# A fourth buffer of split weights, two small copies on another engine, and a mean one step later, in a two-layer hybrid encoder

## The chip, the core and the metric

The kernel runs on one core of a Trainium2 chip. Its engines work side by side, each through a queue of its own: TensorE (matrix products into the accumulation memory PSUM; in the profile PE, its weight loads PEld), VectorE (DVE), ScalarE (ACT), GpSimd (POOL) and SyncE (SP, which here issues most of the loads). The metric is the device time of one execution in microseconds (us); less is better.

## What is computed

Two layers of an encoder over 272 rows (256 tokens and 16 learned meta rows) of width 2048, all in float32. In each layer, shortened from the reference:

```python
proj = h @ w_in                       # gq gk gv gr glr | nq nk nv
y_gla = _gla_mixer(gq, gk, gv, gr, glr, ...)   # 4 heads, both directions, gated by silu(gr)
y_na  = _na_mixer(nq, nk, nv, rel_bias)        # 16 heads, window 4 x 16 of the token grid + 16 meta keys
h = layer_norm(ALPHA * h + concat(y_gla, y_na) @ w_out)
h = layer_norm(ALPHA * h + square(relu(h @ w_ff1)) @ w_ff2)
```

A GLA head's output is divided by the root of its mean square over 256 columns; that mean is the "head's mean" of the title. The keys and values of the neighbourhood attention have 16 columns for the meta rows; these are the "meta columns".

## The kernel before

**Products.** Every product with a weight is made of float32r parts. A weight tile of 128 x 1024 (`raw`, 512 KB from memory) is split by `halves` into a high part (`wh`, a cast on ScalarE, L218) and a low part (`wl`, a subtraction on VectorE, L219). TensorE multiplies high by high, high by the low part of the activations, and low by high. So each of the 768 tiles costs a load, a cast, a subtraction and, in layer 0, 24 matmuls of 272 columns (`eight`, L253). `raw`, `wh` and `wl` are each a ring of three buffers (the pool `wst`, L71). `weights` (L181) hands out the next tile and first sees to it that two tiles are prepared, the one handed out among them.

**Order of the work.** `by_m` (L317) runs one block of 128 output columns after another: for each it takes two or more weight tiles, and after each tile it calls `pump`, after the last one also an eviction of the sum out of PSUM. `by_k` (L279) runs four blocks at once over the pairs of input blocks; it stands at the start of each layer, at the output projection (from `y`, with `mixed` ahead of each pair) and in the first MLP half. The rest of the layer is written as Python generators, which `pump` (L127) steps on between the weight tiles: a foreground queue `fg` (attention pairs, gates) by one step per call, and a background queue `bg` (the four GLA heads, one after another) by a credit per call, 1.3 while the output gates are made (16 calls), 1.4 during the neighbourhood attention. A step that yields True marks the next one as starting with matmuls; such a step is never the second background step of a call, and during the attention it waits up to twice for a marked foreground step (`meet`). Ahead of group 5, the last four blocks of the attention's projection, the background queue is emptied in one go (L405).

The order on each engine's queue is made by the framework's scheduler from this program: earlier instructions first, but one that is ready sooner may be issued ahead. `issue_after(self.wl)` in `step` holds the VectorE instructions of a step behind the newest subtraction L219.

**A GLA head** (`gla_head`, L580) merges keys, queries and decays over levels (L606 on ScalarE, L615 on VectorE, L617 on GpSimd), makes its scores in two groups of small matmuls (L629 to L690), puts them into `A` and `am`, splits these (L339, L340, L345, L346), and multiplies them by the values (L716 to L720: the head's outputs). Squares (L721), their sum (L725) and its split (`mean`, L976) follow; then two matmuls with a constant matrix make the mean (L983), and `newton` the inverse root.

**A pair of attention heads** takes three blocks: query, key, value. `ev_na` (L524) evicts them: a copy of the token columns on ScalarE (L540), one of the meta columns to both halves on VectorE (L541), two small copies on GpSimd (L544). `na_pair` (L762) makes the scores (L778, L782), adds bias and mask (L787, L789, which empty two PSUM banks), takes the softmax (L754 to L760, into `s`, `pr` and, for the meta queries, `sm`), transposes it (L799, L800), turns values (L805 to L808) and sends the probabilities through memory; `na_out` multiplies them (L851) two pairs later. The banks of the scores and of the products come from one ring of four (`pm`).

Of the kernel before, what the change touches and what calls it, by code (L numbers as in the profile page):

```python
# [7 lines left out]
F32 = mybir.dt.float32  # L8
F32R = mybir.dt.float32r
# [5 lines left out]
P = 128  # L15
D = 2048
DC = D // P
T = 256
NM = 16
L = T + NM  # L20
# [8 lines left out]
NK2 = 48  # L29
NKEY = P + NK2  # L30
# [10 lines left out]
WIDE = 1280  # L41
# [17 lines left out]
class Trunk:  # L59
# [24 lines left out]
    def consts(self):  # L84
        nc, c = self.nc, self.cp
        t = lambda n, s, d=F32: c.tile(s, d, name=n, tag=n)
        t("pad", [P, PAD])
        self.vec = t("vec", [P, DEPTH, 66])
        nc.sync.dma_start(self.vec, self.i["vec"].rearrange("l p v -> p l v"))
        self.ident = t("ident", [P, P])  # L90
        nc.sync.dma_start(self.ident, self.i["ident"])
        self.sel = t("sel", [LRK, 2])
        nc.sync.dma_start(self.sel, self.i["sel"])
        self.qmask = t("qmask", [NM, NK2])
        nc.sync.dma_start(self.qmask, self.i["qmask"])
        self.mask = t("mask", [P, 5, 32], U8)
        raw = self.xr.tile([P, 2, L], F32, name="xraw", tag="xraw", bufs=3)[:, 0, :5 * 32].rearrange("p (l c) -> p l c", l=5)
        nc.sync.dma_start(raw, self.i["mask"])
        nc.gpsimd.tensor_copy(self.mask, raw)
        self.ones = {}  # L100
        for n in (GDV, 4 * P, D):
            self.ones[n] = t(f"ones{n}", [P, P])
            nc.gpsimd.memset(self.ones[n], 1.0 / n)
        self.ones_r = {}
        for n in self.ones:
            self.ones_r[n] = t(f"onesr{n}", [P, P], F32R)
            nc.scalar.copy(self.ones_r[n], self.ones[n])
        self.eps = t("eps", [P, 1])
        nc.gpsimd.memset(self.eps, EPS)
        self.one = t("one", [P, 1])  # L110
        nc.gpsimd.memset(self.one, 1.0)
# [68 lines left out]

    def weights(self):  # L181

        while len(self.ready) < 2:
            self.ready.append(self.made(*next(self.stream, (None, (), None))))
        return self.ready.popleft()

    def made(self, ap, ends, kind):
        if ap is None:
            return None
        nc = self.nc  # L190
        raw = self.wp.tile([P, WB], F32, name="raw", tag="raw")
        wh, wl = (self.wp.tile([P, WIDE], F32R, name=nm, tag=nm) for nm in ("wh", "wl"))
        wh, wl = self.blocks(wh, *HIGHS[kind]), self.blocks(wl, *LOWS[kind])
        for c in map(slice, (0,) + ends, ends):
            self.asked = nc.sync.dma_start(raw[:, c], ap[:, c]).ins
            self.halves(raw[:, c], wh, wl, slice(c.start // P, c.stop // P))
        if not ends:
            self.head(ap, raw, wh, wl)
        return wh, wl
# [324 lines left out]
    def ev_na(self, j, ps):  # L524

        nc, m = self.nc, j % 3
        src = ps[:, :T].rearrange("p (r t w) -> p t r w", t=2, r=ROWS)
        if m == 0:
            t = self.a2.tile([P, L], F32, name="nq", tag="nq")
            nc.scalar.mul(t[:, NM:].rearrange("p (t r w) -> p t r w", t=2, r=ROWS), src, NAD ** -0.5)  # L530
            if self.full:
                nc.vector.tensor_scalar(t[:, :NM], ps[:, T:], NAD ** -0.5, None, ALU.mult)
            self.nqkv = [t]
            return
        if m == 1:
            t = self.a2.tile([P, 2, NKEY], F32, name="nk", tag="nk")
            own, rest = t[:, :, :P], t[:, :, P:]
        else:
            t = own, rest = self.nv[j // 3 % 2]
        nc.scalar.copy(own.rearrange("p t (r w) -> p t r w", r=ROWS), src)  # L540
        nc.vector.tensor_copy(rest[:, :, 32:NK2], ps[:, None, T:L].to_broadcast([P, 2, NM]))  # L541
        grid = lambda a: a.rearrange("p (r w) -> p r w", r=ROWS)
        for h, lo in ((0, 0), (1, 24)):
            nc.gpsimd.tensor_copy(grid(rest[:, h, :32]), grid(own[:, 1 - h, :])[:, :, lo:lo + 8])  # L544
        self.nqkv.append(t)
        if m == 2:
            self.y[8 + j // 3] = self.pair(self.yp, "y", 8 + j // 3)
            self.fg.append(self.na_pair(j // 3, *self.nqkv))
            self.wants[self.fg[-1]] = True
# [187 lines left out]
    def na_tiles(self):  # L737

        def t(name, *shape):
            a = self.a2.tile(list(shape), F32, name=name, tag=name, bufs=1)  # L740
            self.nc.gpsimd.memset(a, 0.0)
            return a

        self.fetch = lambda: None
        self.nv = [(self.a2.tile([P, 2, P], F32, name=f"nv{i}", tag=f"nv{i}", bufs=1), t(f"nr{i}", P, 2, 64))
                   for i in range(2)]
        self.npr = [t(f"npr{i}", P, 4, 64) for i in range(2)]
        if self.full:
            self.npm = [t(f"npm{i}", P, 2, NM) for i in range(2)]
            self.nms = [t(f"nms{i}", P, 2, 64) for i in range(2)]  # L750

    def softmax(self, s, st, u, outs, by):
        nc = self.nc
# [8 lines left out]
    def na_pair(self, c, q, k, v):  # L762
        nc, b = self.nc, self.a2
# [2 lines left out]
        bias = b.tile([P, 4, 192], F32, name="nb", tag="nb").rearrange("p u c -> p (u c)")[:, :4 * NKEY]  # L766
        bias = bias.rearrange("p (u c) -> p u c", u=4)
        nc.sync.dma_start(bias, self.i["nab"][self.l, c])
        s = b.tile([P, 4, NKEY], F32, name="ns", tag="ns")
        st = b.tile([P, 12], F32, name="nst", tag="nst")  # L770
        if len(self.due) > 1:
            self.due.popleft()()
        ps = self.spare(2)
        for t in range(2):
            for hh, hs in enumerate(heads):
                for part in heads:
                    at = NM + t * P + part.start
                    nc.tensor.matmul(ps[hh][part, t * NKEY:t * NKEY + NKEY], lhsT=q[hs, at:at + NAD], rhs=k[hs, t, :],  # L778
                                     start=True, stop=True)
        if self.full:  # L780
            for hh, hs in enumerate(heads):
                nc.tensor.matmul(ps[hh][:NAD, 2 * NKEY:2 * NKEY + NK2], lhsT=q[hs, :NAD], rhs=k[hs, 0, P:],  # L782
                                 start=True, stop=True)
            meta = self.nms[c % 2]
            sm = meta[:NM, :, :NK2]
        for hh in range(2):
            nc.vector.tensor_tensor(s[:, 2 * hh:2 * hh + 2, :], two(ps[hh][:, :2 * NKEY]), bias[:, 2 * hh:2 * hh + 2, :], ALU.add)  # L787
            if self.full:
                nc.vector.tensor_tensor(sm[:, hh, :], ps[hh][:NM, 2 * NKEY:2 * NKEY + NK2], self.qmask, ALU.add)  # L789
        pr = self.npr[c % 2]  # L790
        self.softmax(s, st, 4, ((s[:, :, :P], s[:, :, :P]), (pr[:, :, :NK2], s[:, :, P:])), nc.gpsimd)
        yield
        if self.full:
# [26 lines left out]
        p = []  # L820
# [155 lines left out]
    def mean(self, src, n, i=0, pool=None):  # L976

        parts = [t[:, :src.shape[-1]] for t in self.pair(pool or self.lp, "sp", i)]
        self.split(src, *parts)
        yield True  # L980
        p = self.bank()[:, :src.shape[-1]]
        for i, v in enumerate(parts):
            self.nc.tensor.matmul(p, lhsT=self.ones_r[n], rhs=v, start=i == 0, stop=i == 1)  # L983
        return p

    def means(self):
# [140 lines left out]
    def ln_out(self):  # L1127
# [2 lines left out]


        nc, lp, acc = self.nc, self.lp, self.acc
        ident, one = self.ident, self.ones[D]
        t = lambda nm, s, d=F32: lp.tile(s, d, name=nm, tag=nm)
        blocks = [(g, h) for g in range(4) for h in range(2)]
        bank = [self.pm.tile([P, 512], F32, name="mm", tag="mm") for _ in range(4)]
# [145 lines left out]
```

## Time and profile before

| what | us |
|---|---|
| median of 3 runs | 2323.82 (2321.75 to 2325.22) |
| the profiled execution | 2323.91 |
| its span, first to last instruction | 2322.1 |
| TensorE busy | 2304.2 (99%) |
| VectorE busy | 1526.4 (66%) |
| ScalarE busy | 1223.0 (53%) |
| GpSimd busy | 155.4 (7%) |

The profiled execution is 1.8 us longer than its span, and within 0.1 us of the median. A busy TensorE need not be at its peak: a matmul's row in the trace is longer than the distance between the starts of two matmuls, so they overlap. In rows of the timeline stand the start, the length, the engine with its line, what is written from what, its size, and in brackets the idle time before it with what ended it. A line with "q" (SPq, ACTq) is of a queue that issues, not of an engine at work. The granted clock (PEclk) is TensorE's, as a share of its full one.

### The profile page before, as it was taken

The page shows a single profiled execution, that of the slowest core. Times are in us where ns is not written, and L with a number is a line of the kernel's source. Part 1 is how long each engine was busy: PE and PEld are TensorE (multiplying, and loading weights), DVE is VectorE, ACT ScalarE, POOL GpSimd, SP SyncE. Part 2 cuts the span into 40 slices and gives each one's busy share as a digit, 9 for nine tenths or more (in the row PEclk, how much of TensorE's full clock was granted, in tenths as well). Part 3 has the DMA queues.
Part 4 walks back from the last instruction along what each step waited for, and adds up shares of the span by engine and source line. Part 5 has one row for each costly group of instructions (what it writes and reads, how often), then busy time and mean ns, then how long its engine had stood idle before and what let it go on. Part 6 is the DMA issues. An engine that isn't in the chain of part 4 may idle for free.

```text
span 2322.1 us, 45272 instructions
## 1 busy us (share of the span) xinstructions
PE 2304.2 (99%) x18420; PEld 2188.9 (94%) x18420; DVE 1526.4 (66%) x2408; ACT 1223.0 (53%) x2096; POOL 155.4 (7%) x232
## 2 busy tenths in 40 slices
PE   9999999999999999999999999999999999999998
PEld 9999999999999999999999899889988888888888
DVE  5588878875544455547576788688866555666655
ACT  5666655564433344444456766655654334555443
POOL 0023210100000000000020122200100000000000
PEclk9999999999999999999999999999999999999999
DMA  8556666565555556665655556665666666667664
GB/s 259 155 164 184 199 189 177 173 181 181 182 181 178 179 181 182 180 179 178 182 173 173 173 175 209 195 187 181 198 191 196 194 191 193 192 196 218 195 195 150
DMA packets 129824, 431.65 MB, mean 186 GB/s; under 512 B 14792, under 2 KB 23496, under 8 KB 129616
## 3 DMA queue, kind: packets, MB, share of 16 engines
q1 hardware_dynamic: 127024, 421.95, 59.9%
q10 hardware_dynamic: 2592, 6.82, 0.8%
q8 instruction: 144, 2.36, 0.4%
q14 instruction: 64, 0.52, 0.1%
HBM read 420.32 MB, written 8.39 MB: 185 GB/s over the span
## 4 chain that ended last, share of the span: by engine, by line
PE 91%; DVE 5%; ACT 2%; issue 1%; DMA 1%; POOL 0%; DVEq 0%; ACTq 0%; SPq 0%
PE mm L253 53%; PE mm L265 29%; PE mm L304 4%; PE mm L314 2%; DVE wl L219 1%; PE bg L304 1%; ACT wh L218 1%; ACT ns L756 0%; DVE S L615 0%; PE bg L851 0%; PE bg L470 0%; PE bg L629 0%; DVE acc L1085 0%; POOL dec L617 0%; DMA raw<-in_wff 0%
## 5 line engine op out<-in xcount | busy, mean ns | idle before, releaser
L219 DVE TENSOR_TENSOR wl<-raw,wh 128x1024 fp32r<-128x1024 f32 (+1 forms) x770 | 935.9, 1223 | 621.8 <-ACT wh L218 518.5
L218 ACT CAST wh<-raw 128x1024 fp32r<-128x1024 f32 (+1 forms) x770 | 804.7, 1047 | 755.8 <-PE mm L253 352.6
L253 PE MATMUL mm<-x,wh 128*128 128x272 f32 (+3 forms) x4544 | 806.8, 294 | 0.0
L253 PEld LDWEIGHTS mm<-x,wh 128*128 128x128 f32 x4544 | 648.0, 188 | 15.5 <-issue 0.8
L253 PE MATMUL mm<-x,wl 128*128 128x272 f32 (+3 forms) x2432 | 520.6, 285 | 2.9 <-DVE wl L219 2.9
L253 PEld LDWEIGHTS mm<-x,wl 128*128 128x128 f32 x2432 | 391.4, 188 | 3.4 <-DVE wl L219 3.4
L253 PE MATMUL mm<-y,wh 128*128 128x272 f32 (+1 forms) x1440 | 235.0, 285 | 0.0
L253 PEld LDWEIGHTS mm<-y,wh 128*128 128x128 f32 x1440 | 199.7, 188 | 0.1
L265 PE MATMUL mm<-x,wh 128*128 128x512 f32 x832 | 193.8, 390 | 0.0
L265 PEld LDWEIGHTS mm<-x,wh 128*128 128x128 f32 x832 | 154.3, 188 | 31.0
L253 PE MATMUL mm<-u,wh 128*128 128x272 f32 (+1 forms) x1056 | 172.1, 285 | 0.0
L265 PE MATMUL mm<-y,wh 128*128 128x512 f32 x688 | 162.3, 389 | 0.0
L265 PEld LDWEIGHTS mm<-y,wh 128*128 128x128 f32 x688 | 128.7, 188 | 26.8 <-issue 0.4
L253 PE MATMUL mm<-y,wl 128*128 128x272 f32 (+1 forms) x720 | 146.5, 284 | 0.0
L253 PEld LDWEIGHTS mm<-u,wh 128*128 128x128 f32 x1056 | 146.3, 188 | 0.0
L265 PE MATMUL mm<-u,wh 128*128 128x512 f32 x496 | 118.3, 391 | 0.0
L253 PEld LDWEIGHTS mm<-y,wl 128*128 128x128 f32 x720 | 112.5, 188 | 0.0
L265 PEld LDWEIGHTS mm<-u,wh 128*128 128x128 f32 x496 | 90.9, 188 | 17.6
L253 PE MATMUL mm<-u,wl 128*128 128x272 f32 (+1 forms) x528 | 107.4, 284 | 0.0
L265 PEld LDWEIGHTS mm<-x,wl 128*128 128x128 f32 x832 | 98.5, 188 | 2.1
L265 PE MATMUL mm<-x,wl 128*128 128x256 f32 x832 | 99.0, 276 | 0.0
L265 PEld LDWEIGHTS mm<-y,wl 128*128 128x128 f32 x688 | 84.3, 188 | 2.8
(275 smaller groups left out, 2285.0 us busy)
## 6 DMA issues: line engine op xcount, KB each, us to landing
raw<-in_wff SPq DMA_DIRECT2D x512, 512.0 KB, 3.6
raw<-in_win SPq DMA_DIRECT2D x190, 512.0 KB, 4.2
raw<-in_wout SPq DMA_DIRECT2D x64, 512.0 KB, 3.9
hop<-nt ACTq DMA_DIRECT2D x16, 384.0 KB, 2.3
np<-hop SPq DMA_DIRECT2D x64, 96.0 KB, 4.1
nb<-in_nab SPq DMA_DIRECT2D x16, 352.0 KB, 4.4
xraw<-in_xT SPq DMA_DIRECT2D x7, 272.0 KB, 5.8
out<-out SPq DMA_DIRECT2D x5, 256.0 KB, 3.1
```

Of the source, the lines that this page charges most:

```text
L218: self.nc.scalar.copy(h, r)
L219: self.wl = self.nc.vector.tensor_tensor(lo, r, h.bitcast(F32), ALU.subtract).ins
L253: mm(o, lhsT=self.block(w, j), rhs=rhs, start=first and not i, stop=last and i == len(TURNS[once]) - 1)
L265: self.nc.tensor.matmul(o, lhsT=self.block(both[j // 8][low], j % 8), rhs=rhs, start=first and not i + j, stop=bool(last and i and j == 15 ...
L304: self.nc.tensor.matmul(ps[g + m][:, :n], lhsT=self.block(parts[p][0], 4 * j + m if first else 2 * m + j), rhs=acts[k + j][parts[p][1]][:, ...
L314: self.nc.tensor.matmul(o, lhsT=self.block(both[low], i), rhs=rhs, start=not low and k + i % 2 == 0, stop=k == DC - 2 and i % 2 == 1 and n ...
```

## The change

Three edits, and the room for the first.

- `weights` keeps three tiles prepared instead of two; `wh` and `wl` get four buffers. `raw` keeps three.
- The meta columns of keys and values are copied by ScalarE instead of VectorE (L541).
- In `mean`, when a GLA head calls it (`pool` is given), the head yields once more after the split, unmarked, ahead of the step that starts with the two matmuls.
- Room: the constant matrices are kept once, as float32r, and read through a bitcast where float32 is wanted; the scores `s` of a pair, its probabilities `pr` and the meta scores have one buffer instead of two.

```diff
         self.ones = {}
         for n in (GDV, 4 * P, D):
-            self.ones[n] = t(f"ones{n}", [P, P])
-            nc.gpsimd.memset(self.ones[n], 1.0 / n)
-        self.ones_r = {}
-        for n in self.ones:
-            self.ones_r[n] = t(f"onesr{n}", [P, P], F32R)
-            nc.scalar.copy(self.ones_r[n], self.ones[n])
+            one = self.ones[n] = t(f"ones{n}", [P, P], F32R)
+            nc.gpsimd.memset(one.bitcast(F32), 1.0 / n)
+            nc.scalar.copy(one, one.bitcast(F32))
...
-        while len(self.ready) < 2:
+        while len(self.ready) < 3:
...
-        wh, wl = (self.wp.tile([P, WIDE], F32R, name=nm, tag=nm) for nm in ("wh", "wl"))
+        wh, wl = (self.wp.tile([P, WIDE], F32R, name=nm, tag=nm, bufs=4) for nm in ("wh", "wl"))
...
-        nc.vector.tensor_copy(rest[:, :, 32:NK2], ps[:, None, T:L].to_broadcast([P, 2, NM]))
+        nc.scalar.copy(rest[:, :, 32:NK2], ps[:, None, T:L].to_broadcast([P, 2, NM]))
...
-        self.npr = [t(f"npr{i}", P, 4, 64) for i in range(2)]
+        self.npr = t("npr", P, 4, 64)
...
-            self.nms = [t(f"nms{i}", P, 2, 64) for i in range(2)]
+            self.nms = t("nms", P, 2, 64)
...
-        s = b.tile([P, 4, NKEY], F32, name="ns", tag="ns")
+        s = b.tile([P, 4, NKEY], F32, name="ns", tag="ns", bufs=1)
...
-            meta = self.nms[c % 2]
+            meta = self.nms
...
-        pr = self.npr[c % 2]
+        pr = self.npr
...
         self.split(src, *parts)
+        if pool:
+            yield
         yield True
         p = self.bank()[:, :src.shape[-1]]
         for i, v in enumerate(parts):
-            self.nc.tensor.matmul(p, lhsT=self.ones_r[n], rhs=v, start=i == 0, stop=i == 1)
+            self.nc.tensor.matmul(p, lhsT=self.ones[n], rhs=v, start=i == 0, stop=i == 1)
...
-        ident, one = self.ident, self.ones[D]
+        ident, one = self.ident, self.ones[D].bitcast(F32)
```

## The prediction

> **What bounds the kernel now.** I read the page first: the busy times, then the engines' shares of the chain that ended last.
>
> ```profile
> span 2322.1 us, 45272 instructions
> PE 2304.2 (99%) x18420; PEld 2188.9 (94%) x18420; DVE 1526.4 (66%) x2408; ACT 1223.0 (53%) x2096; POOL 155.4 (7%) x232
> PE 91%; DVE 5%; ACT 2%; issue 1%; DMA 1%; POOL 0%; DVEq 0%; ACTq 0%; SPq 0%
> ```
>
> TensorE is the bound, and the change leaves its matmuls as they are. What can be won is time in which it stands still: 2322.1 - 2304.2 = 17.9 us, part of it at the two ends of the span. The view of waits, for TensorE alone, says where the rest lies (us in total, times, longest).
>
> ```profile
> PE bg L983 <- ACT sp L339: 3.3, 3, 1.2
> PE mm L253 <- DVE wl L219: 2.9, 2, 2.3
> PE mm L314 <- DVE nr L541: 0.9, 1, 0.9
> PE mm L304 <- DVE nr L541: 0.8, 1, 0.8
> PE mm L304 <- DVE nms L789: 0.8, 1, 0.8
> PE bg L808 <- DVE nms L760: 0.7, 1, 0.7
> ```
>
> Three kinds of these waits belong to the edits: the head's mean (L983), the low weights (L219) and the meta columns (L541), 3.3 + 2.9 + 0.9 + 0.8 = 7.9 us. I then looked at each in the timeline.
>
> **The fourth buffer.** The longer wait for low weights, in the timeline (start, length, engine, line):
>
> ```profile
> 1452.77 1.04 ACT L218 CAST wh<-raw 128x1024 fp32r<-128x1024 f32 x1
> 1452.97 1.55 DVE L615 TENSOR_TENSOR S<-S,dec 128x256 f32<-128x256 f32 x2 [0.49 <-ACT U L606]
> 1454.44 0.70 DVE L799 STREAM_TRANSPOSE nt<-ns 128x512 f32<-128x512 f32 x1
> 1455.42 0.76 DVE L615 TENSOR_TENSOR S<-S,dec 128x256 f32<-128x256 f32 x2
> 1456.10 1.23 DVE L219 TENSOR_TENSOR wl<-raw,wh 128x1024 fp32r<-128x1024 f32 x1
> 1457.39 0.52 PE L253 MATMUL mm<-x,wl 128*128 128x272 f32 x2 [2.32 <-DVE wl L219]
> ```
>
> The tile's high half came late and its low half stood on VectorE behind a GLA merge and a softmax transposition. Nothing was missing but time: VectorE was busy nearly throughout (a second transposition stands between the rows). Is it the ring of three that holds the preparation back? ScalarE's waits say yes for most of the kernel: its casts wait for TensorE to give a buffer back far more than for a load.
>
> ```profile
> ACT wh L218 <- PE mm L253: 352.6, 212, 2.1
> ACT wh L218 <- DMA raw<-in_wff: 73.4, 62, 2.2
> L253 PE MATMUL mm<-x,wl 128*128 128x272 f32 (+3 forms) x2432 | 520.6, 285 | 2.9 <-DVE wl L219 2.9
> 520.00:560.00 40.00, 40.00 (x330) 40.00 (x329) 22.31 (x28) 18.09 (x27) 0.00 (x0) 1.00 0.59 182
> 1461.96:1467.00 5.04, 5.04 (x42) 5.04 (x42) 0.98 0.76 270
> 1457.39:1461.96 4.57, 4.57 (x24) 4.57 (x25) 0.64 0.61 151
> ```
>
> The last three rows are of windows (length, TensorE busy and its matmuls; granted clock third from the end; the last two rows count the main product alone). A tile of 24 matmuls takes 24 x 40.00 / 330 = 2.9 us. With `weights` keeping three tiles ready and four buffers, a tile may be prepared one such tile earlier: 2.9 us more room, over the 2.32 us that lacked. Both waits go: 2.9 us. With the longer one goes a second loss. Behind it the granted clock was 0.64 while 24 matmuls took 4.57 us; at the next row's rate they take 24 x 5.04 / 42 = 2.9 us, so 1.7 us. Each wait also costs some 0.15 us more than the list says, because a matmul's row (mean 285 ns) is longer than the distance of two starts (0.12 us): 0.3 us. **Term: -4.9 us**, between -4.9 and 0 (the raw ring keeps three buffers; if loads were what came late, nothing goes).
>
> [...]
>
> In a steady stretch nothing changes, as casts still follow the return of buffers at one per tile. What is queued behind them: every step of the GLA and attention work is issued behind the newest low-half subtraction (`issue_after`), which is now one tile further on. Its buffer comes back as early as before (four buffers, one tile further), so I cost this at nothing; without that cover it is one subtraction, 1.23 us, once per stall. At the start the fourth tile's load stands ahead of the second activations' in program order.
>
> ```profile
> 3.54 0.43 SPq L431 DMA_DIRECT2D xraw<-in_xT  x1
> 6.54 2.68 SPq L195 DMA_DIRECT2D raw<-in_win  x2
> ```
>
> That load must wait for a raw buffer until 6.54, while the activations' was free to go at 3.54, and issue order here is not program order (below). I take 0; if SP's queue held it in order, up to 6.54 - 3.54 = 3.0 us less the slack in front, +1 to +3 us.
>
> **The mean one step later.** The three long waits at L983 are 1.13, 1.22 and 0.97 us, two of them at the last head of a layer, one at the first head of layer 1:
>
> ```profile
> 289.99 0.23 PE L690 MATMUL bg<-S,X 128*32 128x16 f32 x6
> 298.06 0.43 DVE L346 TENSOR_TENSOR am<-Am,am 16x272 fp32r<-16x272 f32 x1
> 299.46 0.37 PE L716 MATMUL bg<-parts,V 128*128 128x272 f32 x1
> 301.18 0.29 PE L720 MATMUL bg<-am,VS 80*128 80x272 f32 x1
> 305.12 0.42 ACT L339 CAST sp<-grs 128x272 fp32r<-128x272 f32 x1 [2.23 <-DVE grs L725]
> 305.59 0.87 PE L983 MATMUL bg<-sp,onesr 128*128 128x272 f32 x2 [1.13 <-ACT sp L339]
> 1329.69 0.38 PE L983 MATMUL bg<-sp,onesr 128*128 128x256 f32 x1 [1.22 <-ACT sp L339]
> 1329.91 0.39 PE L253 MATMUL mm<-x,wh 128*128 128x512 f32 x1
> 1485.08 0.84 PE L983 MATMUL bg<-sp,onesr 128*128 128x256 f32 x2 [0.97 <-ACT sp L339]
> ```
>
> A head's outputs end at 301.18 + 0.29 = 301.47, its split lands at 305.12 + 0.42 = 305.54: 4.1 us, over one tile's 2.9 us. Does the new step put a second tile between? I counted the steps by `pump`: 16 calls with credit 1.3, then 40 with 1.4 and the rule of meeting, 17 steps per head before and 18 after; what is left is drained ahead of group 5. In pump calls:
>
> head 1: outputs 11, mean 12; after: 11 and 13.
> head 2: 26 and 29; after: 29 and 30.
> head 3: 40 and 43; after: 43 and 46.
> head 4: 55 and drain; after: both in the drain, one call behind the head's last score matmuls (call 55, before 52).
>
> So the first head gains its tile: in layer 1 that wait goes, 1.22 + 0.15 = **-1.4 us** (layer 0 shows none there). The second head now has one tile in place of three, with the pair's scores before it in the queue: bounds 0 and 1.4 us, I take 0.3 per layer, **+0.6 us**. The last head loses: its outputs need the chain from the score matmuls (290.22) to the split (298.49), 8.3 us, and one tile now lies between instead of three. The last rows but one show what softens it: TensorE's queue isn't in program order (a product of the next tile stands right behind one mean matmul, before the other), so group 5's tiles may be put into the gap, and what is left is by how much the real chain is later than the place it was given. That was 1.13 and 0.97 us for the mean. I take one more such wait per layer, 1.1 + 0.15 each, **+2.5 us**; bounds 0 (fully covered, then the old ones may go as well) and 8.3 - 2.9 = 5.4 us per layer (no tile in the gap). The old waits at the two last heads I leave where they are.
>
> **Meta columns on ScalarE.** 32 copies move, each small:
>
> ```profile
> L541 DVE COPY nr<-mm x16: 173/182/184, 180.5 to 1513.9; 128x32 f32<-128x32 f32 x16
> L696 ACT COPY Am<-bg 16x64 f32<-16x64 f32 x32 | 6.5, 203 | 0.4
> 333.87 0.36 ACT L540 COPY nv<-mm 128x256 f32<-128x256 f32 x1
> 335.14 0.18 DVE L541 COPY nr<-mm 128x32 f32<-128x32 f32 x1
> 335.24 0.43 DVE L862 TENSOR_TENSOR no<-no,bg 128x272 f32<-128x272 f32 x1
> 335.38 0.77 PE L304 MATMUL mm<-y,wh 128*128 128x272 f32 x4 [0.83 <-DVE nr L541]
> 337.48 0.74 PE L304 MATMUL mm<-y,wh 128*128 128x272 f32 x4 [0.83 <-DVE nms L789]
> 240.00:280.00 40.00, 39.38 (x460) 38.73 (x459) 35.40 (x84) 29.09 (x75) 12.90 (x20) 1.00 0.60 180
> ```
>
> VectorE sheds 32 x 0.182 = 5.8 us, ScalarE takes some 32 x 0.2 = 6.4 us (nearest row: L696). In the window, VectorE is busy 35.40 of 40 us and ScalarE 29.09, so the move is the right way round; I cost it at nothing. The bank of the last values is now free at about 334.23 + 0.2 instead of 335.32, and the 0.83 us wait goes. But then TensorE arrives 0.8 us earlier at the score banks, which L789 frees, and VectorE reaches L789 only 0.1 us sooner (L541 lay 335.14 to 335.24 ahead of L862). The stall moves to the row that is already behind it. **Term: -0.1 us per layer, -0.2**; bounds -1.9 (all of 0.8 + 0.9 and the cover) and +0.2.
>
> The rest is room for the fourth buffer and costs nothing: constants kept once in one type (same memsets, casts and matmuls, at the start beside the first loads), one buffer fewer of scores and probabilities. The next pair's scores come at least four pump calls later, 11.7 us, and VectorE, which writes the buffer, is also its last reader.
>
> **Sum:** -4.9 - 1.4 + 0.6 + 2.5 - 0.2 = -3.4 us. The profiled execution took 2323.91 us, 1.8 us more than its span and 0.1 us over the median of the runs, 2323.82. **2323.9 - 3.4 = 2320.5 us.**
>
> **Rivals.**
>
> *All is covered (faster).* Group 5's tiles fill the drain, so that neither new nor old waits of the last heads remain: in place of +2.5 + 0.6 stand -1.13 - 0.97 - 0.3 = -2.4, the rest stays: -4.9 - 1.4 - 2.4 - 0.2 = -8.9, 2315.0 us; with the layer ends' 1.7 us, 2313.3. For it: TensorE's reordering; against it: with one tile ready in the same way both waits were there.
>
> *The drain stalls TensorE to the half clock (slower).* If no tile goes into the last head's gap, each layer waits 5.4 us and then runs 1.7 us slower: 2 x 7.1 = 14.2 in place of 2.5: -3.4 + 11.7 = +8.3, 2332.2 us. It decides once the gap passes the 2.32 us after which the clock fell above; at that point it costs 2 x (2.3 + 1.7) = 8.0 and the sum is +2.1. Against it: the row at 1329.91.
>
> *The buffer does not do what it says.* Loads or the queues' order, not the ring, made the low halves late; only -1.4 + 3.1 - 0.2 = +1.5 us is left, 2325.4. Against it: the late cast followed other work on ScalarE, not a load.
>
> **How the numbers follow.** Forecast 0.55, with 2317 to 2324 as its own range; all covered 0.17; buffer without use 0.13; half clock 0.15. A measurement of this kernel tells some 0.2% from no change, 4.6 us: the runs lie 3.5 us apart. Faster than 2319.2 are the second case and a third of the forecast's: 0.17 + 0.18 = 0.35. Slower than 2328.5 is the half clock: 0.15. Within: 0.50. The range runs from the covered case, 2313.5, past the useless buffer with a late start (+1 to +3), 2328; the half clock is left out.
>
> **What would show it.** Right: no wait at L253 for L219 in the second half of layer 1's attention and no granted clock under 1 there; none at L983 for layer 1's first head; a wait for the outputs (L716 to L720) at each drain; the waits for L541 gone and those at L789 grown. Wrong: a long wait at L716 or L720 with a fallen clock behind it, waits at L219 in new places, or a later third tile at the start.

## The result: 0.47% slower

| | median us | ratio to before, 95% interval |
|---|---|---|
| before | 2323.15 (2321.75 to 2325.22, 6 runs) | |
| changed | 2333.68 (2331.01 to 2336.14, 6 runs) | 1.0047 [1.0036, 1.0057] |

The change costs 10.5 us. The forecast was 2320.5, and the range, 2313.5 to 2328, missed. The profiled execution took 2333.16 us (span 2331.4), 9.3 us more than the one before. Line numbers after the change are lower by 3 in most places: L250 is the main product, L216 the subtraction, L538 the meta copy, L713 to L717 a head's outputs, L336 and L337 a split.

The page after: the busy times and the chain's shares. TensorE has the same 18420 matmuls and is busy 1.8 us longer; the rest of the 9.3 us is standing still.

```profile
span 2331.4 us, 45234 instructions
PE 2306.0 (99%) x18420; PEld 2190.8 (94%) x18420; DVE 1520.3 (65%) x2376; ACT 1227.0 (53%) x2128; POOL 154.1 (7%) x229
PE 91%; DVE 4%; ACT 2%; DMA 1%; issue 1%; POOL 0%; DVEq 0%; SPq 0%; ACTq 0%; POOLq 0%
```

TensorE's waits after (us in total, times, longest):

```profile
PE bg L713 <- ACT parts L336: 8.4, 2, 5.3
PE mm L301 <- DVE nms L786: 2.1, 1, 2.1
PE mm L311 <- DVE ns L784: 1.3, 1, 1.3
PE mm L311 <- ACT nr L538: 1.2, 1, 1.2
PE mm L301 <- ACT x L336: 1.2, 1, 1.2
PE bg L805 <- DVE nms L757: 1.2, 2, 0.7
PE bg L805 <- ACT parts L336: 0.9, 1, 0.9
PE mm L250 <- ACT ft L502: 0.8, 1, 0.8
```

No wait for low weights is left (2.9 us before), and none for a head's mean (3.3 before). In their place the last head's outputs wait 3.1 and 5.3 us, one wait per layer, and every row shown below the first is new or grown. Behind both long waits the clock fell. Windows over the drains of the two layers (length, TensorE busy and its matmuls; granted clock third from the end):

```profile
308.00:311.40 3.40, 3.40 (x15) 3.40 (x16) 2.36 (x3) 2.36 (x6) 0.36 (x2) 0.52 0.00 0
1484.20:1489.90 5.70, 0.41 (x4) 0.19 (x3) 2.28 (x6) 4.90 (x18) 0.00 (x0) 0.91 0.68 226
1489.90:1493.30 3.40, 3.40 (x16) 3.40 (x17) 1.86 (x3) 1.70 (x4) 0.48 (x2) 0.50 0.00 0
```

The clock records give half clock for 3.41 us from 307.87 and for 6.83 us from 1488.88; before, one stretch of 3.41 us from 1458.70 (and in both the end of the kernel).

### The profile page after: what moved, and what is told of

Read it like the earlier page. It is cut to its first block, busy times and chain, and to the rows that moved or that the text cites. A ratio compares the mean times of both kernels' runs of the same rounds, so it can differ in the third digit from the quotient of the medians.

```text
span 2331.4 us, 45234 instructions
## 1 busy us (share of the span) xinstructions
PE 2306.0 (99%) x18420; PEld 2190.8 (94%) x18420; DVE 1520.3 (65%) x2376; ACT 1227.0 (53%) x2128; POOL 154.1 (7%) x229
## 4 chain that ended last, share of the span: by engine, by line
PE 91%; DVE 4%; ACT 2%; DMA 1%; issue 1%; POOL 0%; DVEq 0%; SPq 0%; ACTq 0%; POOLq 0%
PE mm L250 53%; PE mm L262 30%; PE mm L301 3%; PE mm L311 2%; DVE wl L216 2%; DMA raw<-in_win 1%; PE bg L301 1%; ACT wh L215 1%; ACT ns L753 0%; DVE acc L1084 0%; PE bg L848 0%; PE bg L467 0%; PE bg L626 0%; DVE S L612 0%; DVE nst L751 0%
## 5 line engine op out<-in xcount | busy, mean ns | idle before, releaser
L216 DVE TENSOR_TENSOR wl<-raw,wh 128x1024 fp32r<-128x1024 f32 (+1 forms) x770 | 936.5, 1224 | 618.7 <-ACT wh L215 517.6
L250 PE MATMUL mm<-x,wh 128*128 128x272 f32 (+3 forms) x4544 | 807.6, 294 | 0.8 <-ACT ft L502 0.8
L250 PEld LDWEIGHTS mm<-x,wh 128*128 128x128 f32 x4544 | 648.5, 188 | 16.9 <-issue 1.0
L250 PE MATMUL mm<-x,wl 128*128 128x272 f32 (+3 forms) x2432 | 520.1, 284 | 0.0
L250 PEld LDWEIGHTS mm<-x,wl 128*128 128x128 f32 x2432 | 391.3, 188 | 0.0
L250 PE MATMUL mm<-y,wh 128*128 128x272 f32 (+1 forms) x1440 | 235.0, 285 | 0.0
L250 PEld LDWEIGHTS mm<-y,wh 128*128 128x128 f32 x1440 | 199.8, 188 | 0.1
L250 PE MATMUL mm<-u,wh 128*128 128x272 f32 (+1 forms) x1056 | 172.1, 285 | 0.0
L250 PE MATMUL mm<-y,wl 128*128 128x272 f32 (+1 forms) x720 | 146.4, 284 | 0.0
L250 PEld LDWEIGHTS mm<-u,wh 128*128 128x128 f32 x1056 | 146.3, 188 | 0.0
L250 PEld LDWEIGHTS mm<-y,wl 128*128 128x128 f32 x720 | 112.5, 188 | 0.0
L250 PE MATMUL mm<-u,wl 128*128 128x272 f32 (+1 forms) x528 | 107.3, 284 | 0.0
```

Of the source, the lines that this page charges most:

```text
L216: self.wl = self.nc.vector.tensor_tensor(lo, r, h.bitcast(F32), ALU.subtract).ins
L250: mm(o, lhsT=self.block(w, j), rhs=rhs, start=first and not i, stop=last and i == len(TURNS[once]) - 1)
```

## The experiments

Two theories stood after the result. One: the loss is the drain's, waits and fallen clock for the last head's outputs, with the other two edits near zero. The rival: each edit moves the order of the queues and pays for it where other work then stands. Sixteen kernels ran, all with runs of the kernel before on the same chip (medians 2322.89 to 2323.47).

| kernel | median us | ratio to before, 95% interval |
|---|---|---|
| e1: buffers + meta | 2329.51 | 1.0029 [1.0018, 1.0041] |
| e2: late mean alone | 2327.22 | 1.0016 [1.0007, 1.0025] |
| e3: buffers alone | 2323.91 | 1.0004 [0.9995, 1.0013] |
| e4: the change, credit 1.5 | 2330.08 | 1.0027 [1.0017, 1.0037] |
| e5: meta alone | 2329.51 | 1.0029 [1.0019, 1.0039] |
| e6: buffers + late mean | 2327.11 | 1.0017 [1.0009, 1.0026] |
| e7: e3 + values' meta | 2327.54 | 1.0020 [1.0011, 1.0028] |
| e8: e3, two tiles ready at the start | 2322.66 | 0.9999 [0.9990, 1.0007] |
| e9: the change, drains filled | 2331.80 | 1.0035 [1.0021, 1.0049] |
| e10: e8, credit 1.5 | 2323.73 | 0.9999 [0.9990, 1.0008] |
| e11: e1, last values' meta on VectorE | 2328.97 | 1.0026 [1.0015, 1.0037] |
| e12: e8, late mean for the first heads | 2325.70 | 1.0007 [0.9999, 1.0016] |
| e13: e3 + 32 more copies on ScalarE | 2323.49 | 1.0002 [0.9993, 1.0011] |
| e14: e3 without the meta copies | 2330.69 | 1.0033 [1.0020, 1.0045] |
| e15: e3 + keys' meta | 2325.46 | 1.0009 [1.0000, 1.0018] |
| e16: e8, drains filled | 2323.16 | 0.9999 [0.9990, 1.0008] |

### One part at a time (e1, e2, e3)

e1 is the change without the added yield:

```diff
-        if pool:
-            yield
         yield True
```

> The changed kernel without the added step of the mean. Theory (the added step moves the last head's outputs into the drain, and TensorE's waits there and the fallen clock behind them make the loss): waits for the outputs at the drain vanish, the clock stays at 1 there, waits of 1.2 us for the mean come back at the last heads and at layer 1's first head; 2321 to 2324 us. Rival (three prepared tiles and four buffers upset the order of the queues): 2330 us or more.

e2 is the kernel before with that yield alone:

```diff
+        if pool:
+            yield
         yield True
```

> The kernel before with the added step alone. Theory (drain): both drains wait for the outputs by 3 to 5 us, the clock falls behind them, the wait at layer 1's first head goes, those for low weights may stay; 2330 to 2335 us. Rival (buffers): 2321 to 2323 us, since only the first head's wait changes.

e3 is e1 with the meta columns back on VectorE, so that only the buffers and their room are left:

```diff
-        nc.scalar.copy(rest[:, :, 32:NK2], ps[:, None, T:L].to_broadcast([P, 2, NM]))
+        nc.vector.tensor_copy(rest[:, :, 32:NK2], ps[:, None, T:L].to_broadcast([P, 2, NM]))
```

> The kernel before with three prepared tiles, four buffers and the room for them; meta columns on VectorE, mean as before. Theory (drain): both waits for low weights and the fallen clock of layer 1's attention go, 4.9 us, and the start gives 1 us back, since the second activations' load stands behind the fourth tile's; 2319 to 2320.5 us. Rival (buffers): 2328 us or more.

Measured: buffers 2323.91 - 2322.94 = +1.0 us, not to be told from nothing; meta, e1 less e3, +5.6; late mean +4.3 alone and 2333.68 - 2329.51 = +4.2 on top of e1. Each is known to 2 or 3 us. Taken one on top of another they make up the change by construction; measured singly, +1.0, +4.3 and +6.6 (e5 below), they add to 11.9 us against 10.5, which is the same within the noise. All three expectations of the first theory missed: e1 is far above 2324, e2 under 2330, e3 over 2320.5. So the drain is less than half of the loss, and the surprise is the meta copies.

TensorE's waits in e3 show where the fourth buffer's gain went. No row for low weights is there, but the mean's wait at layer 1's last head went from 1.0 to 2.2 us and the outputs ahead of it wait too:

```profile
PE bg L980 <- ACT sp L336: 4.3, 3, 2.2
PE bg L805 <- DVE nms L757: 1.3, 2, 0.7
1477.77 0.38 PE L713 MATMUL bg<-parts,V 128*128 128x256 f32 x1 [0.79 <-ACT parts L336]
1485.45 0.85 PE L980 MATMUL bg<-sp,ones 128*128 128x256 f32 x2 [2.20 <-ACT sp L336]
```

TensorE came earlier to places where the chain through VectorE and ScalarE was not earlier.

In e2 the waits for low weights stay and the drains wait as in the whole change, but less:

```profile
PE bg L716 <- ACT parts L339: 5.1, 2, 2.8
PE mm L253 <- DVE wl L219: 2.8, 4, 1.2
```

### Does the meta copy cost by itself? (e5)

The kernel before with one line changed:

```diff
-        nc.vector.tensor_copy(rest[:, :, 32:NK2], ps[:, None, T:L].to_broadcast([P, 2, NM]))
+        nc.scalar.copy(rest[:, :, 32:NK2], ps[:, None, T:L].to_broadcast([P, 2, NM]))
```

> The kernel before with the meta copies of keys and values on ScalarE and nothing else. Between two kernels that differ in this alone (three tiles ready, mean as before) the edit took 2329.5 - 2323.9 = +5.6 us. Theory A, the copies cost time of their own (ScalarE's queue is on the path of the softmax and of the heads' outputs): +4 to +7 us here too, about 2328.5, with new waits of the nms multiplication and of the score additions. Theory B, the copies change only the order in which the queues are written out, and the price is a matter of which neighbours they meet: another value, anywhere from -2 to +3 us, about 2323.5, with the waits in other places than there.

Measured +6.6 us: theory A by its time and its waits (nms multiplication 1.6 at the first pair, score additions 2.1 and 1.3), though e13 and e14 below refute its reason. The price needs neither of the other edits.

### Do buffers and late mean add up? (e6)

e3 with the yield of e2:

```diff
+        if pool:
+            yield
         yield True
```

> Three tiles ready and the mean one step later, meta columns on VectorE as before. If the edits add up: 2323.9 + 4.2 = about 2328. The wait for the last head's outputs in layer 1 was 2.8 us with the late mean alone and 5.3 us in the whole change. If the third ready tile makes the difference (one more cast of ScalarE and one more subtraction of VectorE ahead of the nq product's copy and addition, behind which the score copies stand): again about 5.3 us and a half-clock stretch of 6.8 us, 2328 to 2330. If the meta copies on ScalarE make it: about 2.8 us and 3.4 us of half clock, 2326 to 2328.

Measured 2327.11, +3.2 over e3 where +4.2 would have been the sum. The wait in layer 1's drain was 3.7 us, between the two expectations: 2.8 with the late mean alone (e2), 3.7 with the buffers as well (e6), 5.3 with the meta copies too (the change). The rows show what sets it. The change, from the last pair's score additions (L784) over its softmax's transposition (L796) and the last score matmul (L683) to the outputs:

```profile
1471.31 2.37 DVE L216 TENSOR_TENSOR wl<-raw,wh 128x1024 fp32r<-128x1024 f32 x2
1473.92 0.51 DVE L784 TENSOR_TENSOR ns<-mm,nb 128x352 f32<-128x352 f32 x1
1479.53 0.71 DVE L796 STREAM_TRANSPOSE nt<-ns 128x512 f32<-128x512 f32 x1 [1.16 <-POOL ns L757]
1480.77 0.24 PE L683 MATMUL bg<-X,S 128*32 128x64 f32 x2
1483.18 0.42 ACT L527 ACTIVATE nq<-jn 128x256 f32<-128x256 f32 x1 [2.86 <-DVE jn L273]
1484.70 0.37 ACT L689 COPY A<-bg 128x256 f32<-128x256 f32 x1
1489.17 0.62 ACT L336 CAST parts<-A 128x512 fp32r<-128x512 f32 x1
1489.84 0.79 PE L713 MATMUL bg<-parts,V 128*128 128x256 f32 x2 [5.29 <-ACT parts L336]
```

The same in e6:

```profile
1469.94 1.23 DVE L216 TENSOR_TENSOR wl<-raw,wh 128x1024 fp32r<-128x1024 f32 x1
1471.51 0.95 DVE L784 TENSOR_TENSOR ns<-mm,nb 128x352 f32<-128x352 f32 x2
1476.87 0.71 DVE L796 STREAM_TRANSPOSE nt<-ns 128x512 f32<-128x512 f32 x1 [1.16 <-POOL ns L757]
1479.76 0.24 PE L683 MATMUL bg<-X,S 128*32 128x64 f32 x2
1487.17 0.51 PE L713 MATMUL bg<-parts,V 128*128 128x256 f32 x2 [3.66 <-ACT parts L336]
```

and in e2:

```profile
1476.59 0.71 DVE L799 STREAM_TRANSPOSE nt<-ns 128x512 f32<-128x512 f32 x1 [1.16 <-POOL ns L760]
1480.24 0.42 ACT L530 ACTIVATE nq<-jn 128x256 f32<-128x256 f32 x1 [2.86 <-DVE jn L276]
1480.33 0.24 PE L686 MATMUL bg<-X,S 128*32 128x64 f32 x2
1486.90 0.51 PE L716 MATMUL bg<-parts,V 128*128 128x256 f32 x2 [2.79 <-ACT parts L339]
```

The chain through VectorE and ScalarE is the same in all three: from the start of the transposition to the outputs it takes 10.3 us, with an attention query's eviction in it (L527, in e2 L530) that waits 2.86 us in the change and in e2. TensorE had one tile of other work in the gap in each. What differs is how far TensorE has come: the scores end 4.0 us after the transposition's start in e2, 3.1 in e6 and 1.5 in the change, and the wait is 6.8 us less that. The buffers bring TensorE there earlier. The meta copies on ScalarE make the chain later: VectorE runs two subtractions ahead of the last pair's score additions, where in e6 it runs one.

### Per copy, or at one place? (e7, e11, e15)

e7 moves only the values' copies, e15 only the keys', both on top of e3:

```diff
+        meta = nc.scalar.copy if m == 2 else nc.vector.tensor_copy
+        meta(rest[:, :, 32:NK2], ps[:, None, T:L].to_broadcast([P, 2, NM]))
```

> Three tiles ready, mean as before, and only the values' meta copies (16 of 32) on ScalarE. With none of them on ScalarE 2323.9, with all 2329.5. A price per copy on ScalarE gives half, 2326.7, with half of each new wait. If the price is that of a changed queue order, it comes whole or not at all: 2323 to 2325 or 2328 to 2330, and the three waits (nms multiplication at the first pair 1.8 us, score addition in layer 0's output product 2.1, clock drop in layer 1's drain 1.7) are each there in full or absent.

> Three tiles ready, mean as before, and only the keys' 16 meta copies on ScalarE. If the prices of keys and values add: 5.6 - 3.6 = +2.0, about 2326, and the wait for the softmax's multiplication at the first pair (1.7 us, there with all copies and absent with the values' alone) is in it. If each copy costs alike: +2.8, 2326.7. If the two are not separate, since either half changes the order once: +3 to +5, 2327 to 2329.

e11 is e1 with the last values of each layer back on VectorE:

```diff
-        nc.scalar.copy(rest[:, :, 32:NK2], ps[:, None, T:L].to_broadcast([P, 2, NM]))
+        meta = nc.vector.tensor_copy if j == 23 else nc.scalar.copy
+        meta(rest[:, :, 32:NK2], ps[:, None, T:L].to_broadcast([P, 2, NM]))
```

> Three tiles ready, mean as before, meta copies on ScalarE except those of the last head's values in each layer (30 of 32 moved). With all 32 on ScalarE it took 2329.5, with none 2323.9; the values' 16 alone 2327.5. If the values' price is made at one place, the output product, where TensorE's banks wait for the last values' copy and the score additions behind it: the 2.3 and 1.4 us waits for these additions fall back to two waits of about 1 us in each layer's place, the half clock there goes, and about 2326 is left (the keys' part). If each copy on ScalarE has its share: 2329.2.

Measured: values +3.6, keys +1.6, together 5.2 against 5.6 for all. e7 is neither the half nor the whole that was expected; e15 met its first figure, but not the wait that was to be in it (1.7 us at the first pair; it has 0.8 at most). e11 missed: 2328.97, not 2326. Its wait for the score additions fell from 2.1 to 0.8 us, but the copy ahead of them waited 1.1 again and in layer 1 the copy's wait grew to 1.5. So the price was not made by that one copy, and it grew with the number of copies moved: 16, 30 and 32 cost 1.6 to 3.6, 5.1 and 5.6 us, not far from their time on ScalarE (32 x 0.187 = 6.0). That looks like ScalarE's time. It is not, as the next two show.

### ScalarE's time or VectorE's order? (e13, e14)

e13 leaves the copies on VectorE and gives ScalarE 32 more; e14 leaves them out and lets GpSimd write zeros in their place.

```diff
+        idle = self.a2.tile([P, 2, NM], F32, name="idle", tag="idle")
+        nc.scalar.copy(idle, ps[:, None, T:L].to_broadcast([P, 2, NM]))
         nc.vector.tensor_copy(rest[:, :, 32:NK2], ps[:, None, T:L].to_broadcast([P, 2, NM]))
```

```diff
-        nc.vector.tensor_copy(rest[:, :, 32:NK2], ps[:, None, T:L].to_broadcast([P, 2, NM]))
+        nc.gpsimd.memset(rest[:, :, 32:NK2], 0.0)
```

> Three tiles ready, mean as before, meta copies on VectorE as before, and besides them 32 copies of the same columns on ScalarE into a tile that nobody reads. Measured so far against 2323.9 with no copy on ScalarE: 16 give +3.6, 30 +5.1, 32 +5.6, near their own time there (0.185 us each, 5.9 in all). If ScalarE's time is what the copies cost: +5 to +6 here as well, about 2329.5, with the wait for the softmax's multiplication at the first pair (1.7 us). If the price comes from what VectorE then does in their place (another order of its queue): 2323 to 2325.

> Three tiles ready, mean as before, and the meta columns of keys and values set to zero by GpSimd instead of copied: their copy is left out of VectorE and given to nobody (GpSimd is busy 7%). If ScalarE's time is the price: faster than or equal to 2323.9 by VectorE's 5.8 us at most, 2320 to 2324. If VectorE's changed order is the price: it comes here too, 2326 to 2330, with the waits at the score additions of the output product grown to 2 us.

This decides between the two. 32 more copies on ScalarE cost nothing (2323.49, 0.4 us under e3). Taking 32 copies of 0.18 us off VectorE costs +6.8 us (a little over the range), though no engine copies them now, and the new waits are those of e1 and e5, which have no zeros from GpSimd: 1.6 us at the first pair, 2.2 and 1.4 at the output products. The price is that of the order in which the work is then done. The traces show the change of order. Leave the 32 copies aside and count how few of VectorE's 2376 other instructions must be moved to make two traces alike: 30 between e1 and e3, 7 between e14 and e1, none between e13 and e3. So e13 has e3's order and e3's time, and e14 has nearly e1's order and its time. ScalarE's order changes along with VectorE's (22 of 2096 between e1 and e3, 20 between e14 and e3, none between e13 and e3), and no run separates the two; the rows below and those of e6 above show VectorE's.

What the new order does at the first pair of attention heads, first in e3:

```profile
217.06 0.12 DVE L754 RECIPROCAL mst<-mst 16x2 f32<-16x2 f32 x1
217.21 0.24 DVE L757 TENSOR_TENSOR nms<-nms,mst 16x96 f32<-16x96 f32 x1
219.04 0.27 PE L805 MATMUL bg<-ident,nms 128*128 128x128 f32 x1
219.35 0.70 DVE L796 STREAM_TRANSPOSE nt<-ns 128x512 f32<-128x512 f32 x1
```

and in e14:

```profile
218.37 1.04 POOL L757 TENSOR_TENSOR ns<-ns,nst 128x512 f32<-128x512 f32 x1
218.71 0.15 DVE L754 RECIPROCAL mst<-mst 16x2 f32<-16x2 f32 x1 [0.46 <-ACT nms L753]
219.44 0.71 DVE L796 STREAM_TRANSPOSE nt<-ns 128x512 f32<-128x512 f32 x1 [0.57 <-POOL ns L757]
220.08 0.26 DVE L757 TENSOR_TENSOR nms<-nms,mst 16x96 f32<-16x96 f32 x1
220.48 0.30 PE L805 MATMUL bg<-ident,nms 128*128 128x128 f32 x1 [1.63 <-DVE nms L757]
```

In e3 the small multiplication for the meta queries, which TensorE waits for, comes ahead of the large transposition; in e14 it stands behind it, and the transposition waits for GpSimd. A multiplication of 0.26 us so costs TensorE 1.63, about 1.2 of it by standing there; the whole softmax is also later in e14. The multiplication's input was ready at 218.86 (218.71 + 0.15), 1.2 us before it ran at 220.08, so VectorE did not take it ahead of the transposition here, though it stood idle for 0.57 us of that time.

### The start (e8)

```diff
-        self.stream, self.ready = self.order(), deque()
+        self.stream, self.ready, self.deep = self.order(), deque(), 2
...
-        while len(self.ready) < 3:
+        while len(self.ready) < self.deep:
...
                         first = self.by_k(self.x, L, self.load_x, wide=True)
+                        self.deep = 3
```

> Three tiles ready, mean as before, meta on VectorE, but only two ready during the first product of layer 0. The first 40 us of the profile with three ready hold 1.7 us more of waits than the kernel before (4.15 against 2.34 + their small parts). If these come from the third tile's load standing ahead of the activations' on the load queue: -1.3 to -1.8 us against 2323.9, about 2322.3, and the stretch as in the kernel before. If they come from the third tile's cast and subtraction or from chance: no change, 2323.9.

Measured 2322.66, 1.25 us under e3, as expected though inside the two intervals. After the first matmul e8's profile has no wait of TensorE in the first 40 us, where e3's has one of 0.70 at 18.96 and the change's one of 1.19 at 11.93. But e3's profile also got the full clock only at 6.95 us and e8's at 4.52, so the two stretches differ by more than the load. With that the buffers alone give 0.2 us less than before, which is no difference.

### The drain and the clock (e4, e9, e16)

e4 is the change with a credit of 1.5, by which nothing is left for the drain:

```diff
-GLA_R, GLA_NA, NORMS = 1.3, 1.4, (1.0, 0.6)
+GLA_R, GLA_NA, NORMS = 1.3, 1.5, (1.0, 0.6)
```

> The changed kernel with a background credit of 1.5 instead of 1.4 per call during the attention. By the count of steps the means then stand at calls 13, 29, 43 and 55 and nothing of a head's matmuls is left for the drain, with the added step kept. Theory (drain): no wait for outputs or mean in the drains, no fallen clock there; 2319 to 2322 us. Rival (the step itself, or the buffers): 2330 us or more.

Measured 2330.08, 3.6 us under the change, and the rival's figure. The drain waits went, but the denser steps put the score matmuls ahead of their operands (3.4 us for merged operands at L626, 1.7 at L678), the softmax's waits are back at 2.9 us (e1 has 3.2, the change 1.2), and the clock fell for 10.2 us elsewhere (mean over this execution 0.997).

e9 puts matmuls that nobody reads into the change's drains, e16 into e8's (8 and 16, ahead of the last heads' means):

```diff
             o = self.bank()[:, :n]
+            for _ in range((24, 40)[self.l] if h == GH - 1 and not e else 0):
+                nc.tensor.matmul(o, lhsT=self.ones[GDV], rhs=self.x[0][0][:, :n], start=True, stop=True)
```

> The whole change, with matmuls that compute nothing needed (24 in layer 0, 40 in layer 1, 2.9 and some 4.7 us at 0.12 us each) ahead of the last head's outputs, written into a bank that the outputs then overwrite from their start. In the whole change TensorE waits there 3.0 and 5.3 us and then runs 3.4 and 6.8 us at half the clock, in which some 1.6 and 3.2 us are lost. If the fallen clock is a cost of its own that follows from the idle time: the waits shrink to under 1 us, the half clock behind them goes, and the kernel takes 4 to 5 us less, 2329. If the idle time alone costs and the clock falls for another cause: no gain, 2333 to 2334, with the half clock still there. If the filling matmuls are put elsewhere or run over the wait: slower than 2334.

> The fastest version so far (three tiles ready, two during the first product, meta on VectorE, mean as before: 2322.66), with 8 and 16 matmuls that compute nothing needed ahead of the last heads' means in layers 0 and 1 (1.0 and 1.9 us of them, in waits of 1.3 and 2.3). The clock fell behind the longer wait in that version's profile and not in another one's with a wait as long. If idle time inside one clock window is what makes it fall: no half clock in layer 1's drain and about 1 to 1.7 us less, 2321 to 2322. If filling changes nothing there: 2322.7. If the fillers stand in the way: 2323.5 or more.

In e9 the waits shrank to 0.4 and 0.7 us and the half clock in both drains went, so the fall does follow from the idle time. The gain was 1.9 us, inside the two intervals, not 4 to 5: the filler takes some 64 x 0.12 = 7.7 us, a little more than the waits left for it, and in this execution the clock fell at two other waits (3.41 us each, at the output products; mean 0.998). In e16 the half clock of e8's drain went too (the granted clock was 1.00 from 1479.21 to 1486.04), with no gain that can be told: layer 1's output product then waited 2.2 us where it had waited 0.9.

### Other ways to keep the gain (e10, e12)

e10 is e8 with the credit line of e4. e12 is e8 with the yield for the first head only:

```diff
-        ms = yield from self.mean(rs, GDV, pool=g2)
+        ms = yield from self.mean(rs, GDV, pool=g2, late=not h)
...
+        if late:
+            yield
         yield True
```

> Three tiles ready (two during the first product), meta on VectorE, mean as before, and a credit of 1.5 in place of 1.4 per step in the attention's product, by which the last head's mean comes in step 55 and nothing is left for the drain (counted: last scores 49, outputs 52, mean 55). If the drain waits cost what they show (1.3 and 2.3 us with 1.7 us of clock) and nothing takes their place: 2322.7 - 4.5 = 2318. If denser steps bring waits at the score matmuls as they did in the whole change with 1.5 (3.4 us for the gathered operands, 2.9 for the softmax): about 2322 to 2325.

> Three tiles ready (two during the first product), meta on VectorE, and the mean one step later for each layer's first head only. By the count of steps the last head stays where it was before (scores 52, outputs 55, mean in the drain). If all the late mean's price lies in the drain and its gain at layer 1's first head is real: that wait (1.16 us) goes, no wait for the last head's outputs comes, 2322.7 - 1.3 = 2321.4. If a step more disturbs the order as such: 2324 or more, with new waits at the second head.

e10: 2323.73. Its drain waits are gone; 2.3 us for merged operands (L627), 1.8 us for those of L679 and 6.8 us of half clock at 1458 (mean 0.998) came in their place. e12 missed, 2325.70 for 2321.4. Layer 1's first-head wait went and the drains stayed as they were, both as counted, but the third heads' score matmuls wait for their merged operands (S, X and U, 2.9 us in all) and the clock fell for 6.8 us at the first of these waits (235.41 us; mean 0.997). By the count of steps the third head's last merge comes in call 36 instead of 34, since the second head ends later, and its score matmuls in call 37 as before: one tile of room in place of three. No version here beats the kernel before by what a measurement can tell.

## Why the prediction was wrong, point by point

The forecast was -3.4 us and the measurement +10.5. Term by term: -4.9 became +1.0, +1.7 became +4.2, and -0.2 became +5.6. Most of the signs that were named for being right came all the same (no wait for low weights, none for the mean of layer 1's first head, a wait for the outputs at each drain, those at L789 grown), and so did one of those for being wrong (a long wait for the outputs with a fallen clock behind it). None of them looked at the order of VectorE's work.

**The bound** was read rightly: TensorE bounds both kernels (busy 99% of either span), and the losses found are waits of it or a slower clock (0.50 at its lowest).

**Fourth buffer, -4.9.** The waits at L253 for L219 and the clock behind the longer one went, as said. The step that failed is that nothing else would move ("the old waits at the two last heads I leave where they are"): by e3 the term is +1.0, and its interval (-1.2 to +3.0) leaves -4.9 out. Part was given back within 30 us of the gain (the mean 1.0 to 2.2, the outputs 0 to 0.8), part at the start, which I took as 0 with a bound of +1 to +3. SP's rows after:

```profile
2.12 4.94 SPq L192 DMA_DIRECT2D raw<-in_win  x4
7.11 0.43 SPq L428 DMA_DIRECT2D xraw<-in_xT  x1
11.93 1.26 PE L301 MATMUL mm<-x,wh 128*128 128x272 f32 x8 [1.19 <-ACT x L336]
```

The activations' load, at 3.54 before, stood behind the fourth tile's until 7.11, and TensorE waited 1.2 us: SP did issue in program order here, and the price is at the lower end of the bound. e8's 1.25 us fits that, without proving it.

**Mean later, +1.7 in all** (-1.4 + 0.6 + 2.5). Measured +4.3 alone, +4.2 in the change. The count of steps was right, the first head's wait in layer 1 went, and the second head's 0.6 did not come (0.2 us stands at the third head's outputs in layer 0, and 0.9 at a softmax matmul, L805, just ahead of them). Mis-sized is the drain: the prediction said that group 5's tiles "may be put into the gap" and took 1.1 us per layer. TensorE took none beyond the one tile that already lay between. Layer 1's wait, 5.3 us, is the upper bound worked out there (5.4); layer 0's is 3.1; with the late mean alone (e2) they are 2.8 and 2.3. With the half clock behind them (0.50 from 307.87 and from 1488.88) this is the slower rival's mechanism, which I gave 0.15. That its figure, +8.3 and 2332.2 us, lies near the measured 2333.68 is luck: it charges 14.2 us to the drains, where the late mean cost 4.2 in all, and nothing to the meta copies, which cost 5.6. The row that I set against it, at 1329.91, shows a product between two mean matmuls, so that TensorE's order had been written that way; that a gap is filled as it comes, it does not show, and in the drains none was.

**Meta columns, -0.2.** Measured +5.6, outside its bounds (-1.9 to +0.2), and the largest miss with the buffers. The failing step: "the move is the right way round; I cost it at nothing", because VectorE was the busier engine. Busy shares do not price a move: e13 shows that ScalarE had the room, e14 that VectorE without the copies is the slower one, since its other work then runs in another order (30 instructions moved). The forecast that the stall of the output product moves to the row behind it held (L789 0.8 to 2.1), as did its size roughly: 2.1 in place of 0.8 + 0.8. In layer 1 the copy's own wait, which was to go, stayed in the change at 1.2 us. The copies also cost where the prediction did not look: at the first pair (1.6 us in e1, e5 and e14, though 0.5 in the change, where the late step has moved things again) and in layer 1's drain (3.7 to 5.3 us).

**What is not settled.** Why the scheduler writes the slower order when the copies go was not tried, only that it does; which engine's order costs how much was not separated; the waits that e14's profile shows over e3's (1.6 at the first pair, 2.2 and 1.4 for the score additions of the two output products, less the waits that these replaced) make 3.5 us of span at full clock. Its other five executions are 2.6 to 5.5 us longer, at a mean clock of 0.997 or 0.998, so the median's rest goes with the clock.

## What to carry to other kernels

Where a scheduler writes each engine's queue, an edit is also a new order on engines that it hardly touches: test a moved instruction by its two halves, added there and left out here, before believing either engine's load. A wait that goes is worth something only until the next place where the same consumer meets a chain that did not get faster; look 30 us further before adding it to the sum. When one step is put into a paced background queue, the last one of the round falls off its end: count where that one lands, and compare when its consumer and its producers get there: here the wait was what the consumer was ahead, and no other work filled it.

## What the runs showed of the hardware

In the executions before and after, every change of the granted clock on record lies on a grid of 3.413 us. Before, the clock was full from 4.63 us and half from 1458.70 (426 steps of 3.413 us on) for 3.41 us and from 2318.86 (678 steps) to the end. After, it was full from 4.08 and half from 307.87 (89 steps) for 3.41 us, from 1488.88 (435) for 6.83 us and from 2328.56 (681) to the end. Windows on these grids, before first and then after (length, TensorE's busy time first, clock third from the end):

```profile
1455.29:1458.70 3.41, 1.31 (x10) 1.31 (x11) 3.31 (x8) 2.83 (x7) 0.66 (x2) 1.00 0.50 135
1458.70:1462.11 3.41, 3.41 (x17) 3.41 (x16) 2.64 (x4) 1.72 (x4) 0.00 (x0) 0.50 0.64 195
304.46:307.87 3.41, 0.48 (x4) 0.26 (x3) 0.14 (x2) 3.19 (x13) 0.00 (x0) 1.00 0.79 285
307.87:311.28 3.41, 3.28 (x14) 3.28 (x15) 2.27 (x3) 2.37 (x7) 0.36 (x2) 0.50 0.00 0
1482.05:1485.47 3.42, 2.50 (x21) 2.29 (x19) 1.99 (x3) 2.27 (x7) 0.00 (x0) 1.00 0.87 258
1485.47:1488.88 3.41, 0.00 (x0) 0.00 (x0) 1.02 (x5) 2.68 (x11) 0.00 (x0) 1.00 0.75 240
1488.88:1492.29 3.41, 2.45 (x11) 2.45 (x12) 2.02 (x3) 2.29 (x5) 0.48 (x2) 0.50 0.02 8
1492.29:1495.71 3.42, 3.42 (x17) 3.42 (x17) 1.37 (x4) 1.13 (x3) 0.00 (x0) 0.50 0.45 153
```

TensorE stood idle for 2.10, 2.93 and 3.41 us of the windows ahead of the three half-clock stretches that lie before the ends. In the first window of the stretch of 6.83 us it was idle again, for 0.96 us; in those of 3.41 us for 0.00 and 0.13 us. The other 18 windows of full clock in which it was idle for more than 0.6 us (0.61 to 1.34 us; away from the first 20 us and the ends) were followed by full clock. So the same wait need not have the same price. e3 and e1 both wait 2.2 us for the mean in layer 1's drain. In e3 the windows that follow from its full clock at 6.95 us (432 steps of 3.413 us on) cut the wait into 1.67 and 0.61 us, and the clock stays:

```profile
1481.51:1484.92 3.41, 1.74 (x15) 1.52 (x13) 3.12 (x6) 1.82 (x5) 0.00 (x0) 1.00 0.81 228
1484.92:1488.34 3.42, 2.81 (x20) 2.62 (x21) 2.39 (x6) 2.42 (x5) 1.14 (x2) 1.00 0.62 232
```

In e1 2.26 us of idle time lie in one window, and the clock of the next is 0.50:

```profile
1485.92:1489.33 3.41, 1.15 (x7) 0.73 (x6) 2.54 (x6) 1.75 (x5) 0.00 (x0) 1.00 0.92 298
1489.33:1492.74 3.41, 3.41 (x18) 3.41 (x17) 3.18 (x6) 1.24 (x5) 1.14 (x2) 0.50 0.59 168
```

What idle times between 1.67 and 2.10 us in one window do, these windows do not show. Where a wait lies on such a grid may also be why one program's executions differ, but that was not shown, since only the profiled ones have clock records: e14 took a span of 2324.9 us at a mean clock of 1.000 and 2329.8 at 0.997 (mean of three). The wait of 2.2 us had two prices in two profiles, and a single profile shows one of them.
